# The S5 Toeplitz matrix of a hybrid mixer, laid out by DMAs that shift partitions in place of matmuls with shift matrices

## The chip, the cores and the metric

The kernel runs on one core of a Trainium2 chip. The metric is device time in microseconds of one execution, lower is better. The kernel before was timed three times: 862.27, 859.94 and 861.67 us, so its median is 861.67 us.

## What is computed

One layer of a hybrid block, batch 1, 512 tokens, width 1024, all in float32: an adaptive layer norm whose six rows come from `c @ w_ada`, an input projection, two branches (a four-head mLSTM and a 512-wide S5 state-space model), a gated mix, a second adaptive norm and a convolutional GLU of hidden width 2816. The change lies in the S5 branch alone:

```python
def _s5_ssm(u, lam_re, lam_im, log_dt, b_re, b_im, c_re, c_im, d):
    ...                                   # ar, ai = exp(lam*dt); bb = B scaled by (a-1)/lam
    bu_r = einsum('bsgc,gpc->bsgp', ug, bbr)          # 32 groups of 16 channels, 64 states
    bu_i = einsum('bsgc,gpc->bsgp', ug, bbi)
    ...                                   # x[s] = a * x[s-1] + bu[s], complex, along the 512 tokens
    y = einsum('gcp,bsgp->bsgc', c_re, xr) - einsum('gcp,bsgp->bsgc', c_im, xi)
    return y.reshape(B, S, W) + d * uf
```

The kernel cuts the 512 tokens into 64 blocks of 8. Inside a block the answer to the block's own inputs is a product with a block-Toeplitz matrix, whose 16x16 blocks are K[t-s] = C A^(t-s) B for t >= s and zero otherwise.

## The kernel before

Every large product (input projection, GLU of the S5 branch, mLSTM down projection, mix, FFN up and down) runs as three fp32r matmuls: `mm3` (L241 to L244) multiplies the high part of the weights with the high and the low part of the activations, and the low part of the weights with the high part. A weight tile of 128x1024 is loaded by SP into tag `w` (2 buffers), rounded to fp32r by ACT into `wh` (L221, through `split_into`), and the rest goes into `wl` by a DVE subtraction (L210). One such tile makes 24 matmuls of 512 columns.

The mixer stage is a list of tokens, `SEQ` (L144 to L150), written out by hand: `k` is one step of the first projection, `u x o g l d` a weight tile of 24 matmuls, `S` one step of the S5 stream and `H` one step of the mLSTM head stream. So S5 and head work is interleaved with weight tiles. Python order gives the priority; a list scheduler then orders the instructions of each engine at build time, so an instruction of a later token can stand a few places ahead of one that is not ready. On the chip each engine takes its own instructions strictly in that order. SP issues all DMAs, in one order.

The S5 stream is `s5_scalars`, and then for each quarter q of the groups `s5_params(q)` and `s5_run(q)`:

- `s5_params`, by S steps. (1) load B and C, build AB by DVE products (`cmul`). (2) G = AB transposed. (3) K: 16 matmuls (L523), an ACT copy (L524), a transpose (L525), an ACT cast into K high (L527) and a DVE subtraction into K low (L210); then the Toeplitz matrix TT: for each of 8 rows t one 0/1 shift matrix of 128x128 times K high and K low (L534, L535), into two PSUM banks of tag `s5`, each emptied by an ACT copy (L536). (4) F by DVE products. (5) E, the powers for the scan, by DVE and POOL.
- `s5_run`: (6) eight DMAs write the inputs into U (L575 to L577, shown as L192). (7) G times U (L583), a scan on DVE. (8) products on DVE into XB, then py = F times XB (L612) plus TT times U (L614), and an ACT copy (L617). (9) eight DMAs back (L621, L622), the skip term and gelu.

The shift matrices are an input of 512 KB (`in_shift`), loaded once and cast once by ACT (L501), and they hold one of the five `s5b` buffers until the fourth TT. TT is first read at L614, five S steps after it is made. The tiles of tag `s5b` (5 buffers) in a quarter are AB, G, TT and F.

Of the kernel before, what the change touches and what calls it, by code (L numbers as in the profile page):

```python
# [16 lines left out]
P = 128  # L17
# [37 lines left out]
def pack(i):  # L55
    f = np.float32
    a = {k: np.asarray(v) for k, v in i.items()}
    o = {}
    o["x"] = a["x"][0]
    wa = a["w_ada"][0].reshape(KD, P, 6, KD, P)  # L60
    o["wa1"] = wa[:, :, [1, 0]].transpose(3, 1, 0, 2, 4).reshape(KD, P, KD * 2 * P)
    o["wa2"] = wa[:, :, [4, 3, 2, 5]].reshape(KD, P, 4 * D)
    perm = np.arange(S).reshape(4, KD, C5).transpose(0, 2, 1).reshape(-1)
    w_in = a["w_in"][0]
    b_in = a["b_in"][0]
    o_i = 2 * D
    o_us = o_i + 8
    o_ga = o_us + S
    gg = np.arange(2 * D).reshape(2, KD, P).transpose(1, 0, 2).reshape(-1) + o_ga
    order = np.concatenate([o_us + perm, np.arange(o_i), gg])  # L70
    wt = w_in[:, order].reshape(KD, P, 36, P)
    bmain = b_in[order]
    o["w0"] = wt[:, :, :NXM0].reshape(KD, P, NXM0 * P)
    o["win"] = wt[:, :, NXM0:].transpose(2, 1, 0, 3).reshape(36 - NXM0, P, D)
    wg = np.zeros((KD, P, 32), f)
    wg[:, :, :8] = w_in[:, o_i:o_us].reshape(KD, P, 8)
    o["wg"] = wg.transpose(1, 0, 2).reshape(P, KD * 32)
    wq = a["w_mlstm_q"][0].reshape(2, 2, 2, P, QK)
    wk = a["w_mlstm_k"][0].reshape(2, 2, 2, P, QK)
    o["wqk"] = np.stack([wq, wk], 2).transpose(0, 4, 1, 2, 3, 5).reshape(2, P, D)  # L80
    o["wdn"] = a["w_mlstm_down"][0].reshape(KD, P, KD, P).transpose(2, 1, 0, 3).reshape(KD, P, D)
    o["wglu"] = a["w_s5_glu"][0][perm].reshape(4, P, 2, KD, P).transpose(3, 1, 2, 0, 4).reshape(KD, P, D)
    o["wmix"] = a["w_mix_out"][0].reshape(KD, P, D)
    o["wup"] = a["w_ffn_up"][0].reshape(KD, P, 2, NF, P).transpose(3, 2, 1, 0, 4).reshape(2 * NF, P, D)
    o["wfd"] = a["w_ffn_down"][0].reshape(NF, P, D)
    cols = np.zeros((P, NCOLS), f)

    def put(name, v):
        s, n = COLS[name]
        cols[:, s:s + n] = v  # L90

    ada = a["b_ada"][0].reshape(6, KD, P)
    put("c", a["c"][0].reshape(KD, P).T)
    put("ada1", ada[[1, 0]].transpose(2, 0, 1).reshape(P, 16))
    put("ada2", ada[[4, 3]].transpose(2, 0, 1).reshape(P, 16))
    put("b_in", bmain.reshape(36, P).T)
    put("b_gate", np.broadcast_to(b_in[o_i:o_us], (P, 8)))
    put("cw", a["w_mlstm_conv"][0].reshape(4, KD, P).transpose(2, 0, 1).reshape(P, 32))
    put("cb", a["b_mlstm_conv"][0].reshape(KD, P).T)
    put("gain", a["mlstm_norm_gain"][0].reshape(KD, P).T)  # L100
    put("d", a["s5_d"][0][perm].reshape(4, P).T)
    put("fw", a["w_ffn_conv"][0].reshape(3, NF, P).transpose(2, 0, 1).reshape(P, 66))
    put("fb", a["b_ffn_conv"][0].reshape(NF, P).T)
    o["rows"] = np.stack([ada[2].reshape(-1), ada[5].reshape(-1), a["ln1_gain"][0], a["ln1_bias"][0],
                          a["ln2_gain"][0], a["ln2_bias"][0]])
    lam = np.zeros((P, 3, NG), f)
    lam[:, 0] = a["s5_lam_re"][0].reshape(NG, P).T
    lam[:, 1] = a["s5_lam_im"][0].reshape(NG, P).T
    lam[:, 2] = np.repeat(a["s5_log_dt"][0].reshape(NG, 2).T, N5, 0)
    o["lam"] = lam.reshape(P, 3 * NG)  # L110
    bc = np.stack([np.stack([a["s5_b_re"][0], a["s5_b_im"][0]]),
                   np.stack([a["s5_c_re"][0], a["s5_c_im"][0]]).transpose(0, 1, 3, 2)])
    o["s5bc"] = bc.reshape(2, 2, 4, 4, P, C5).transpose(4, 2, 0, 1, 3, 5).reshape(P, 4, 256)
    o["ident"] = np.eye(P, dtype=f)
    mk = np.zeros((P, 16), f)
    mk[np.arange(16), np.arange(16)] = 1.0
    mk[32 + np.arange(16), np.arange(16)] = 1.0
    put("mask", mk)
    sg = np.zeros((P, 8), f)
    for j in range(8):  # L120
        sg[j::32, j] = 1.0
    put("selg", sg)
    o["cols"] = cols
    sh = np.zeros((P, T5, P), f)
    for t in range(T5):
        for s in range(t + 1):
            for q in range(C5):
                sh[(t - s) * C5 + q, t, (T5 - 1 - s) * C5 + q] = 1.0
    o["shift"] = sh.reshape(P, T5 * P)
    return {k: np.ascontiguousarray(v) for k, v in o.items()}  # L130


# [26 lines left out]
def _build(ctx, tc, nc, h):  # L159
# [19 lines left out]
    def big(shape=(P, D), dt=F32, tag="hb"):  # L179
        return tl(tag, shape, dt)  # L180
# [304 lines left out]
        tt(dst, x, c[:, 0:1, g4][:, :, :, None].to_broadcast([P, 2, 4, m]))  # L485
        tt(dst, dst, t, ALU.add)

    shr = [None]

    def s5_params(q, out):  # L490
        g4 = slice(4 * q, 4 * q + 4)
        bc = s5h()
        dma(bc[:, :256], h["s5bc"][:, q, :])
        b4 = bc.rearrange("p (x r a c) -> p x r a c", x=4, r=2, a=4)
        bt, ct = b4[:, 0], b4[:, 1]
        cb = bc[:, 256:].rearrange("p (r a c) -> p r a c", r=2, a=4)
        if shr[0] is None:
            s_ = big(tag="s5b")
            dma(s_, h["shift"])
            shr[0] = big((P, T5, P), F32R, "s5b")  # L500
            A.copy(shr[0].rearrange("p a b -> p (a b)"), s_)  # L501
        AB = big((P, 2, 4, P), tag="s5b")
        cmul(AB[:, :, :, :C5], bt, prm["z"], g4, False, C5)
        for i, a_ in enumerate(prm["apow"]):
            n = C5 << i
            cmul(AB[:, :, :, n:2 * n], AB[:, :, :, :n], a_, g4, False, n)
        yield
        gts(ct[:, 1], ct[:, 1], -1.0)
        GP.memset(cb, 0.0)
        GP.tensor_copy(cb[0:64, :, :, 0:C5], ct[0:64])  # L510
        GP.tensor_copy(cb[64:P, :, :, C5:32], ct[64:P])
        G = big((P, 2, 4, P), tag="s5b")
        for ri in range(2):
            pg = bank("s5")
            for i in range(4):
                T.transpose(pg[:, i * P:(i + 1) * P], AB[:, ri, i, :], ident)
            A.copy(G[:, ri].rearrange("p a b -> p (a b)"), pg)
        yield
        kt = s5h(P)
        pk = bank("s5")  # L520
        for ri in range(2):
            for i in range(4):
                T.matmul(pk[32 * i:32 * i + 32, :P], lhsT=cb[:, ri, i, :], rhs=AB[:, ri, i, :], start=ri == 0, stop=ri == 1)  # L523
        A.copy(kt, pk[:, :P])  # L524
        T.transpose(pk[:, P:2 * P], kt, ident)  # L525
        K = s5h(256, F32R).rearrange("p (a b) -> p a b", a=2)
        A.copy(K[:, 0, :], pk[:, P:2 * P])  # L527
        sub(K[:, 1, :], pk[:, P:2 * P], f32(K[:, 0, :]))
        TT = big((P, 8, T5, C5), tag="s5b")
        for b in range(2):  # L530
            pq = bank("s5")
            for i in range(4):
                o = pq[:, i * P:(i + 1) * P]
                T.matmul(o, lhsT=shr[0][:, 4 * b + i, :], rhs=K[:, 0, :], start=True, stop=False)  # L534
                T.matmul(o, lhsT=shr[0][:, 4 * b + i, :], rhs=K[:, 1, :], start=False, stop=True)  # L535
            A.copy(TT[:, :, 4 * b:4 * b + 4, :], pq.rearrange("p (t g c) -> p g t c", t=4, c=C5))  # L536
        yield
        F = big((P, 2, 4, P), tag="s5b")
        cmul(F[:, :, :, :C5], ct, prm["apow"][0], g4, True, C5)
        for i, a_ in enumerate(prm["apow"]):  # L540
            n = C5 << i
            cmul(F[:, :, :, n:2 * n], F[:, :, :, :n], a_, g4, True, n)
        yield
        E = s5h().rearrange("p (r g k) -> p r g k", r=2, k=K5)
        t = s5h().rearrange("p (r g k) -> p r g k", r=2, k=K5)
        lo8, hi8 = prm["e8"]
        E5, t5 = (x.rearrange("p r g (i l) -> p r g i l", l=8) for x in (E, t))
        for ri in range(2):
            lv = [lo8[:, k, g4, None, :].to_broadcast([P, 4, 8, 8]) for k in (ri, 1 - ri)]
            hv = [hi8[:, k, g4, :, None].to_broadcast([P, 4, 8, 8]) for k in range(2)]  # L550
            tt(E5[:, ri], lv[0], hv[0])
            tt(t5[:, ri], lv[1], hv[1])
            tt(E[:, ri], E[:, ri], t[:, ri], ALU.add if ri else ALU.subtract)
        rho = s5h().rearrange("p (r g k) -> p r g k", r=2, k=K5)
        GP.tensor_copy(rho, prm["m8"][:, None, g4, None].to_broadcast([P, 2, 4, K5]))
        GP.memset(rho[:, :, :, 0:1], 0.0)
        out[q] = (TT, G, F, E, rho)
        yield
# [698 lines left out]
```

## Time and profile before

| what | value |
|---|---|
| timed runs (device time) | 862.27, 859.94, 861.67 us, median 861.67 us |
| span of the profiled execution | 862.0 us |
| PE busy | 828.5 us (96%), 4106 matmuls |
| DVE busy | 607.1 us (70%) |
| ACT busy | 368.6 us (43%) |
| POOL busy | 98.0 us (11%) |
| mean granted TensorE clock | 0.994 |
| HBM traffic | 101.01 MB read, 2.10 MB written |

The profiled execution has its span and no other time of its own; the span stands 0.33 us above the median of the timed runs, inside their spread, so nothing measurable lies around it. PE's 96% is a share over the whole span, and matmuls are pipelined; so what PE waits for, and which engine the chain of work runs through, has to be read stretch by stretch. The S5 quarters lie between about 60 and 300 us.

### The profile page before, as it was taken

The numbers are of one execution on the slowest core, as the hardware profiler recorded it, in microseconds if no ns is written. First come the engines' busy times: TensorE is split into PE (matmuls) and PEld (weight loads), VectorE is DVE, ScalarE is ACT, GpSimd is POOL, SyncE is SP. The second block draws the span as 40 slices with busy tenths as digits, with TensorE's granted clock in tenths as the row PEclk, the third lists the DMA queues.
The fourth block names the chain that finished last, engine by engine and source line by source line (L and its number), as shares of the span: only waits on it lengthen the run. The fifth ranks groups of instructions, "written<-read, shape, count | busy, mean of one in ns | idle before, by whom it ended". The sixth has DMA issues, their size and how long they took to land.

```text
span 862.0 us, 11353 instructions
## 1 busy us (share of the span) xinstructions
PE 828.5 (96%) x4106; PEld 669.2 (78%) x4106; DVE 607.1 (70%) x1144; ACT 368.6 (43%) x589; POOL 98.0 (11%) x255
## 2 busy tenths in 40 slices
PE   3999999999999999999999999999999999999996
PEld 1777868778777778888887988888888878888785
DVE  5557978788689774578978767556777675878144
ACT  4454573564556442232334555444444444333000
POOL 2781211122022100000002200000000000000000
PEclk9999999999999999999999999999999999999998
DMA  9832132122222233568655023224444232445011
GB/s 336 288 132 86 53 101 62 45 85 62 79 60 87 86 123 122 196 203 294 210 191 177 2 74 102 94 98 147 146 147 137 86 120 74 171 163 169 11 49 49
DMA packets 45415, 105.94 MB, mean 123 GB/s; under 512 B 13360, under 2 KB 14256, under 8 KB 45360
## 3 DMA queue, kind: packets, MB, share of 16 engines
q1 hardware_dynamic: 45360, 105.23, 36.0%
q8 instruction: 32, 0.52, 0.2%
q14 instruction: 23, 0.19, 0.1%
HBM read 101.01 MB, written 2.10 MB: 120 GB/s over the span
## 4 chain that ended last, share of the span: by engine, by line
PE 76%; DVE 11%; ACT 4%; DMA 4%; issue 2%; SPq 2%; POOL 0%; DVEq 0%; ACTq 0%; POOLq 0%
PE acc L242 11%; PE acc L243 11%; PE acc L244 11%; PE hd L242 11%; PE hd L243 11%; PE hd L244 11%; DVE hh L202 2%; SPq L192 2%; DVE s5h L207 1%; PE s L242 1%; PE s L244 1%; PE s L243 1%; DVE wl L210 1%; PE s L612 1%; DMA w<-in_wmix 1%
## 5 line engine op out<-in xcount | busy, mean ns | idle before, releaser
L221 ACT CAST wh<-w 128x1024 fp32r<-128x1024 f32 (+2 forms) x103 | 103.2, 1003 | 144.0 <-PE acc L243 111.5
L210 DVE TENSOR_TENSOR wl<-w,wh 128x1024 fp32r<-128x1024 f32 (+2 forms) x103 | 120.5, 1172 | 60.8 <-ACT wh L221 60.1
L242 PE MATMUL acc<-hp,wh 128*128 128x512 f32 x256 | 103.4, 405 | 0.5 <-ACT hx L785 0.5
L244 PE MATMUL acc<-hp,wl 128*128 128x512 f32 x256 | 102.1, 399 | 0.0
L243 PE MATMUL acc<-hp,wh 128*128 128x512 f32 x256 | 102.1, 399 | 0.0
L242 PE MATMUL hd<-s5b,wh 128*128 128x512 f32 (+1 forms) x168 | 63.4, 380 | 0.7 <-ACT s5b L1169 0.5
L243 PE MATMUL hd<-s5b,wh 128*128 128x512 f32 (+1 forms) x168 | 63.6, 379 | 0.2 <-DVE s5b L210 0.2
L244 PE MATMUL hd<-s5b,wl 128*128 128x512 f32 (+1 forms) x168 | 63.3, 378 | 0.0
L242 PEld LDWEIGHTS acc<-hp,wh 128*128 128x128 f32 x256 | 48.2, 189 | 14.7 <-issue 3.7
L202 DVE SCALAR_TENSOR_TENSOR hh<-hh,hh 128x512 f32<-128x512 f32 x52 | 35.9, 691 | 31.2 <-ACT hh L564 14.7
L244 PEld LDWEIGHTS acc<-hp,wl 128*128 128x128 f32 x256 | 48.4, 189 | 11.2 <-issue 0.4
L243 PEld LDWEIGHTS acc<-hp,wh 128*128 128x128 f32 x256 | 48.4, 189 | 10.8 <-issue 0.4
L202 DVE SCALAR_TENSOR_TENSOR s5h<-hh,k,s5h 128x512 f32<-128x512 f32 x56 | 39.3, 746 | 4.7 <-DMA hh<-in_wa 4.6
L242 PEld LDWEIGHTS hd<-s5b,wh 128*128 128x128 f32 x168 | 31.3, 188 | 7.6 <-ACT s5b L1169 0.8
L243 PEld LDWEIGHTS hd<-s5b,wh 128*128 128x128 f32 x168 | 31.7, 189 | 7.0 <-DVE s5b L210 0.6
L244 PEld LDWEIGHTS hd<-s5b,wl 128*128 128x128 f32 x168 | 31.6, 188 | 6.4
L202 DVE SCALAR_TENSOR_TENSOR hh<-hh,k,hh 128x512 f32<-128x512 f32 x44 | 33.0, 751 | 4.5 <-ACT hh L1186 3.6
L1024 POOL TENSOR_SCALAR mov<-mov 128x1 f32<-128x1 f32 x6 | 3.7, 624 | 276.2 <-ACT s L1023 159.6
L244 PE MATMUL acc<-hx,wl 128*128 128x512 f32 x84 | 33.1, 394 | 0.0
L242 PE MATMUL acc<-hx,wh 128*128 128x512 f32 x84 | 33.1, 394 | 0.0
L243 PE MATMUL acc<-hx,wh 128*128 128x512 f32 x84 | 33.1, 394 | 0.0
L244 PE MATMUL acc<-s5b,wl 128*128 128x512 f32 x80 | 31.6, 395 | 0.5 <-DVE wl L210 0.5
(547 smaller groups left out, 2053.1 us busy)
## 6 DMA issues: line engine op xcount, KB each, us to landing
w<-in_wup SPq DMA_DIRECT2D x44, 512.0 KB, 3.2
hh<-in_wa SPq DMA_DIRECT2D x64, 256.0 KB, 4.2
w<-in_win SPq DMA_DIRECT2D x30, 512.0 KB, 3.2
w<-in_wfd SPq DMA_DIRECT2D x22, 512.0 KB, 3.3
hb<-in_wa SPq DMA_DIRECT2D x16, 512.0 KB, 7.4
w<-in_wglu SPq DMA_DIRECT2D x8, 512.0 KB, 3.3
w<-in_wdn SPq DMA_DIRECT2D x8, 512.0 KB, 3.3
w<-in_wmix SPq DMA_DIRECT2D x8, 512.0 KB, 4.2
```

What stands on the lines that cost most here:

```text
L192: return nc.sync.dma_start(o, i)
L202: V.scalar_tensor_tensor(o, i0, s, i1, op0=op0, op1=op1)
L207: V.tensor_tensor(o, a, b, op=op)
L210: V.tensor_tensor(o, a, b, op=ALU.subtract)
L221: A.copy(hi, x)
L242: T.matmul(o, lhsT=wh, rhs=xh, start=first, stop=False)
L243: T.matmul(o, lhsT=wh, rhs=xl, start=False, stop=False)
L244: T.matmul(o, lhsT=wl, rhs=xh, start=False, stop=last)
L612: T.matmul(o, lhsT=F[:, ri, pr, :], rhs=XB[:, ri, pr].rearrange("p g k -> p (g k)"), start=ri == 0, stop=False)
L1024: GP.tensor_scalar(v[:, 2:3], v[:, 0:1], v[:, 1:2], EPS * D, op0=ALU.add, op1=ALU.add)
```

## The change

The shift input, its load, its cast and the 64 matmuls with it are gone. K is now one plain float32 tile (no high and low part). For each t an SP DMA copies rows 0 to 127-z of K to rows z to 127 of a new tile TR at place t, with z = 16(7-t), and POOL zeroes the first z rows (seven memsets a quarter, none for t = 7). Then the S step ends (the `yield` stands behind the DMAs), and the next S step begins with one ACT copy of 128x1024 from TR into TT, which changes the order of the free dimensions from (t, group, channel) to (group, t, channel), and goes on with F. The number of S steps is the same. TR is a fifth `s5b` tile of a quarter, in the place of the shift matrices' buffer.

```diff
-    sh = np.zeros((P, T5, P), f)
-    ...
-    o["shift"] = sh.reshape(P, T5 * P)
...
-        if shr[0] is None:
-            s_ = big(tag="s5b")
-            dma(s_, h["shift"])
-            shr[0] = big((P, T5, P), F32R, "s5b")
-            A.copy(shr[0].rearrange("p a b -> p (a b)"), s_)
...
-        K = s5h(256, F32R).rearrange("p (a b) -> p a b", a=2)
-        A.copy(K[:, 0, :], pk[:, P:2 * P])
-        sub(K[:, 1, :], pk[:, P:2 * P], f32(K[:, 0, :]))
+        K = s5h(P)
+        A.copy(K, pk[:, P:2 * P])
+        TR = big((P, T5, 8, C5), tag="s5b")
+        for t in range(T5):
+            z = (T5 - 1 - t) * C5
+            if z:
+                GP.memset(TR[0:z, t], 0.0)
+            dma(TR[z:P, t].rearrange("p g c -> p (g c)"), K[0:P - z, :])
+        yield
         TT = big((P, 8, T5, C5), tag="s5b")
-        for b in range(2):
-            pq = bank("s5")
-            for i in range(4):
-                o = pq[:, i * P:(i + 1) * P]
-                T.matmul(o, lhsT=shr[0][:, 4 * b + i, :], rhs=K[:, 0, :], start=True, stop=False)
-                T.matmul(o, lhsT=shr[0][:, 4 * b + i, :], rhs=K[:, 1, :], start=False, stop=True)
-            A.copy(TT[:, :, 4 * b:4 * b + 4, :], pq.rearrange("p (t g c) -> p g t c", t=4, c=C5))
-        yield
+        A.copy(TT.rearrange("p g t c -> p t g c"), TR)
```

## Rows read from the trace of the kernel before

**Rows 1.** Busy time by stretch: length, then PE, PEld, DVE, ACT, POOL, clock, DMA, GB/s.
```profile
100.00:150.00 50.00, 48.41 (x274) 39.52 (x274) 42.55 (x101) 25.72 (x46) 9.27 (x23) 1.00 0.26 82
...
300.00:350.00 50.00, 49.47 (x214) 39.35 (x215) 29.97 (x41) 18.65 (x24) 0.00 (x0) 1.00 0.36 122
```

**Rows 2.** Who PE waited for, whole span: total us, times, longest us.
```profile
PE s L612 <- DVE k L210: 3.3, 3, 1.7
```

**Rows 3.** The shift matmuls by line, and two pieces of the chain of work through them.
```profile
L535 PE MATMUL s<-s5h,s5b x32: 223/274/327, 67.0 to 252.4; 128*128 128x128 f32 x32
...
67.23 0.11 PE s L534
```

**Rows 4.** ACT by line: the two copies out of PSUM in each quarter.
```profile
L536 ACT COPY s5b<-s x8: 581/587/590, 67.9 to 253.3; 128x512 f32<-128x512 f32 x8
```

**Rows 5.** DMA issues: size of each, median us from issue to landing.
```profile
w<-in_win SPq DMA_DIRECT2D x30, 512.0 KB, 3.2
...
s5h<-hx SPq DMA_DIRECT2D x32, 32.0 KB, 2.1
...
s5b<-in_shift SPq DMA_DIRECT2D x1, 512.0 KB, 5.8
```

**Rows 6.** SP's issues in order of time, by start and length.
```profile
67.42 5.83 SPq L192 DMA_DIRECT2D s5h<-hx  x8
...
295.27 1.95 SPq L192 DMA_DIRECT2D hh<-in_wa  x4
```

**Rows 7.** What SP's queue and ACT's weight casts waited for, whole span.
```profile
SPq L192 <- DVE wl L210: 427.5, 89, 36.0
...
ACT wh L221 <- PE acc L243: 111.5, 39, 5.8
```

**Rows 8.** POOL in order of time: a memset of 64 columns.
```profile
67.92 0.15 POOL L671 MEMSET hh<- 128x64 f32 x1
```

**Rows 9.** DVE in order of time, first quarter; in brackets the idle time before.
```profile
66.54 0.29 DVE L210 TENSOR_TENSOR s5h<-s,s5h 128x128 fp32r<-128x128 f32 x1 [0.50 <-ACT s5h L527]
...
74.98 0.19 DVE L652 TENSOR_TENSOR k<-hd,k 128x32 f32<-128x32 f32 x1 [0.49 <-PE hd L650]
```

**Rows 10.** ACT in order of time, first quarter.
```profile
69.31 1.20 ACT L769 ACTIVATE hx<-hd,k 128x512 f32<-128x512 f32 x1
...
73.10 0.59 ACT L647 COPY hh<-hd 128x512 f32<-128x512 f32 x1 [0.36 <-PE hd L645]
79.51 1.05 ACT L221 CAST wh<-w 128x1024 fp32r<-128x1024 f32 x1 [5.83 <-PE acc L243]
```

**Rows 11.** Second quarter, DVE in order of time.
```profile
129.52 0.29 DVE L202 SCALAR_TENSOR_TENSOR hh<-hd,hh 128x128 f32<-128x128 f32 x1 [0.66 <-POOL hh L854]
...
144.06 1.29 DVE L207 TENSOR_TENSOR hh<-hd,hx 128x512 f32<-128x512 f32 x2 [0.16 <-PE hd L891]
```

**Rows 12.** Second quarter, PE in order of time: the wait ahead of L612.
```profile
161.61 0.46 PE L612 MATMUL s<-k,s5b 128*128 128x128 f32 x2 [1.65 <-DVE k L210]
```

**Rows 13.** Third quarter: DVE in order of time, then PE ahead of L612.
```profile
190.32 0.29 DVE L210 TENSOR_TENSOR s5h<-s,s5h 128x128 fp32r<-128x128 f32 x1 [0.25 <-ACT s5h L527]
...
202.51 1.29 DVE L207 TENSOR_TENSOR hh<-hd,hx 128x512 f32<-128x512 f32 x2 [0.42 <-PE hd L891]
...
222.67 0.73 PE L612 MATMUL s<-k,s5b 128*128 128x128 f32 x4 [1.24 <-DVE k L210]
```

**Rows 14.** Fourth quarter: DVE, then PE, in order of time.
```profile
250.68 0.72 DVE L198 TENSOR_SCALAR hh<-hh,mmv,ms 128x256 f32<-128x256 f32 x2
...
253.47 1.08 DVE L210 TENSOR_TENSOR s5b<-hx,s5b 128x512 fp32r<-128x512 f32 x1 [0.68 <-ACT s5b L221]
...
252.54 0.63 PE L891 MATMUL hd<-k,hh 128*128 128x128 f32 x4
```

**Rows 15.** Busy time behind two waits ahead of L612; clock third from the end.
```profile
163.00:166.00 3.00, 3.00 (x16) 3.00 (x16) 2.98 (x4) 0.00 (x0) 0.00 (x0) 0.50 0.06 12
...
222.00:224.00 2.00, 1.33 (x11) 1.36 (x12) 1.96 (x5) 0.00 (x0) 0.00 (x0) 1.00 0.66 250
```

## What the change will do to the time, predicted before it ran

> **What bounds the kernel now.** I read the busy time by stretch first. Between 100 and 150 us PE is busy 48.4 of 50 us and DVE 42.6; between 300 and 350 us PE 49.5 and DVE 30.0 [rows 1]. So PE is the bound, but in the S5 stage DVE stands close behind it, while later it doesn't. Then the list of PE's waits: the one of the S5 stage that returns is L612, which waits for the last DVE subtraction into XB, 3.3 us in three waits [rows 2]. There PE has run out of work that it may do before DVE is through. That decides how this change is to be costed: PE work that is taken away in front of such a wait comes back as a longer wait, unless the DVE work in between starts earlier too. So for each quarter I follow DVE from the shift matmuls to L612 and look for the idle time that PE had caused. Only that idle time, and work that leaves DVE itself, can be won.
>
> **What is removed from PE.** 32 matmuls on L534 and 32 on L535, one every 0.11 us in the chain of work [rows 3]: 64 x 0.11 = 7.0 us, 1.76 us in each quarter. This is the ceiling of the gain from PE.
>
> **Where it arrives, quarter by quarter.** The low part of K leaves DVE too: one subtraction of some 0.2 to 0.3 us a quarter.
> - First quarter. DVE waits 0.50 us for the cast of K (L527) and then subtracts; both go, and F starts 0.7 us earlier. From there DVE works without a break on F, E and a weight tile until L652 of the gates, ahead of which it idles 0.49 us waiting for PE [rows 9]. With PE 1.8 us earlier that wait goes too. Gain 0.7 + 0.5 = 1.2 us.
> - Second quarter. From 129.52 us DVE is busy with F, E, the statistics of the head and weight tiles, and the only idle time on the way to L612 that ends with PE is 0.16 us, before 144.06 [rows 11]. Gain 0.16 us; PE's wait ahead of L612 grows from 1.65 us [rows 12] to about 3.2.
> - Third quarter. The wait for the cast (0.25 us) and the subtraction (about 0.2) go, and the 0.42 us in which DVE waits for PE's L891 [rows 13]. Gain 0.9 us; the wait ahead of L612 grows from 1.24 us [rows 13] to about 2.1.
> - Fourth quarter. The last four transposes of L891 start at 252.54 us, behind the shift matmuls, though DVE had made their input by 250.68 + 0.72 = 251.40 [rows 14]: PE could win 1.1 us, and 0.3 more by the missing subtraction. DVE idles 0.68 us behind an ACT cast that had stood behind L536 [rows 14]; with the subtraction that is 1.0 us. I take the smaller, 1.0 us, since DVE is full behind it.
>
> Sum: 1.2 + 0.16 + 0.9 + 1.0 = 3.3 us. After 300 us PE has no such neighbour, and what was won stays won.
>
> **What goes at no price.** The load of 512 KB (5.8 us to landing [rows 5]) and its one cast on ACT lie ahead of the first quarter, in a stretch where PE works on; I book nothing, at most some tenths of a microsecond. The two PSUM banks of tag `s5` a quarter come free earlier; nothing.
>
> **What is added.** (1) SP: 8 issues a quarter. The trace has no such DMA. The nearest issues from SBUF to SBUF, U's, take 5.83 us for eight [rows 6], 0.73 each; plain loads take 1.95 us for four, 0.49 each [rows 6]. So 3.9 to 5.8 us of SP a quarter, and the landing 2.1 us behind the last issue [rows 5]. The first waits for the copy of K; behind it in SP's queue stand U's eight DMAs and the next weight loads. In the first quarter U would be issued from about 71 us on in place of 67.42, but L583 reads it at 87. The weight loads have room: SP stood 427 us in all waiting for DVE to free a `w` buffer, and the casts waited 111 us for PE to free `wh` [rows 7], so a load that starts 4 us later is still early. I book nothing; a price of up to 1 us in all stays in the range.
>
> (2) ACT: one copy of 128x1024 in place of two of 0.587 us [rows 4]. A cast of the same size took 1.05 us [rows 10], so 1.05 to 1.2 us against 1.17: nothing. But it waits for the DMAs, and ACT takes its work in order. In the first quarter K is there at 66.5 us [rows 9], the last DMA lands between 66.5 + 7 x 0.49 + 2.1 = 72.0 and 66.5 + 7 x 0.73 + 2.1 = 73.7 us. Behind the copy could stand L769 (69.31), L647 of the gates (73.10) and, after an idle stretch of 5.8 us, the cast at 79.51 [rows 10]. If the copy stands in that idle stretch it costs nothing, and since TT is read only near 101 us, that is where I put it. If it stands just ahead of L647, it holds the gates until 73 to 75 us and the 1.2 us of the first quarter are lost, with up to 1.7 more. I take nothing, and keep both ends.
>
> (3) POOL: seven memsets a quarter of 128 columns. 64 columns took 0.15 us [rows 8], so 0.2 to 0.3 us each, 1.4 to 2.1 us a quarter. DVE does wait for POOL's masks at times (0.66 us before 129.52 [rows 11]); if memsets fall just there, some of it is added: 0 to 1 us in all.
>
> The Trainium skill speaks against such a change: "DMA: Bandwidth & Descriptors", Rules for kernel authors, says to coalesce many small transfers, since under 64 KB one pays mostly overhead. The trace agrees as far as it goes: 32 KB land in 2.1 us and 512 KB in 3.2 [rows 5]. By that rule alone the 32 DMAs would be all latency; it turns into time only if someone waits for them, which is the second rival.
>
> **The sum.** 861.67 - 3.3 = 858.4 us. The sum is made against a span of 862.0 us (858.7 after it); the median lies 0.33 us below the span, so I subtract from the median. With the unknown costs of SP, POOL and ACT the forecast's own range is 857.5 to 861.
>
> **The rivals.**
> - The whole PE time arrives: 861.67 - 7.0 = 854.7 us. It needs DVE's order to move so that the head and scan operations come ahead of F and E, which nobody needs until L612 and the scan. The scheduler could do that, since PE would hand over the heads' results earlier. For it: F and E stand between in all quarters. Against it: in the second quarter DVE is full whatever the order.
> - Slower: the copy into TT stands on ACT right behind the copy of K, and ACT stands still for the DMAs. In the first quarter that holds ACT from 66.5 to 73.7 us, then the copy, so L769, which empties the PSUM bank for the gates' matmuls, starts at 74.8 in place of 69.31 [rows 10]. PE has no other work ready between the last step of the first projection and the gates, and loses 5.5 us less the idle time of its own, about 4.9; the other three quarters still bring 0.16 + 0.9 + 1.0 = 2.1. That gives 861.67 + 4.9 - 2.1 = 864.5 us; if the same happens in the second quarter, where ACT's exponentials lead to POOL's masks and DVE [rows 11], 4 to 5 us more, 869. It decides as soon as the copy stands ahead of L769 there. For it: the two S steps of the first quarter follow each other without a token between. Against it: U's and the back DMAs' readers wait little, so the scheduler knows roughly how long eight DMAs take.
> - The clock: the waits ahead of L612 grow to 2 and 3 us. After the wait of 1.65 us in the second quarter the granted clock was 0.50, the 1.2 GHz level, through the stretch from 163 to 166 us, where 16 matmuls took 3.0 us [rows 15], 0.19 each in place of 0.11 [rows 3]; after the 1.24 us of the third it stayed at 1.00 [rows 15]. One more such stretch costs about half of 3.4 us, 1.7 us: 858.4 + 1.7 = 860.1, two 861.8 us.
> - It doesn't do what it says: no case for that; the matmuls are gone from the program.
>
> On the clock the Trainium skill ("TensorE: Matmul & The Clock Gate", HAM oscillation) says that idle gaps of PE take the clock to half and that this cost is paid anew for each. The rows agree for one gap and not for the other [rows 15]; what a gap of 2 us does is shown by none.
>
> **Chances.** Forecast (857.5 to 861, most of it under 859.1) 0.42; whole PE time (853.5 to 857) 0.2; clock 0.17; ACT stands still (863 to 870) 0.13; small losses that leave 859 to 862, 0.08. The likeliest time is 858.4. The range leaves out the deep end of the slower case and little of the fast one: 854 to 863 us. A measurement of this kernel tells about 0.3%, 2.6 us, from no change: faster means below 859.1, slower above 864.3. Faster: 0.42 x 0.75 + 0.2 = 0.52; slower 0.11; the rest, 0.37, the same.
>
> **What would show it.** Right: PE busy falls by about 7 us; PE's waits for DVE at L612 grow from 3.3 us to some 6 to 7; L652 of the gates comes 1 to 2 us earlier, and the stage after the fourth quarter about 3 us earlier. ACT's copy into TT starts without a wait of more than a microsecond or two. Wrong: L612's waits stay as they were and the S5 stage ends 6 to 7 us earlier (first rival); ACT idle for DMAs by 3 us or more ahead of the copy, with PE idle behind it (second); a second stretch of clock 0.50 between 60 and 300 us (third).

## The result, and the profile after

The changed kernel took 894.97 us (median, 893.20 to 895.72), the kernel before 861.08 us in the same comparison: a ratio of 1.039, 95% interval 1.0375 to 1.0404. So it is 33.9 us slower, where 858.4 us and a range up to 863 had been forecast.

The profiled execution of the changed kernel took 893.2 us and has a span of 891.2; some 2 us lie around the span. The prediction had the span of before alone and saw nothing around it. By spans the loss is 891.2 - 862.0 = 29.2 us; the rest of the 33.9 between the medians lies in how the two profiled executions stand to their medians. The next lines, both of the changed kernel, are the busy times and one stretch (length, PE, PEld, DVE, ACT, POOL, clock, DMA, GB/s).

```profile
PE 831.6 (93%) x4042; PEld 668.6 (75%) x4042; DVE 604.8 (68%) x1140; ACT 367.9 (41%) x584; POOL 101.9 (11%) x283
```

```profile
300.00:350.00 50.00, 30.65 (x140) 24.50 (x139) 25.19 (x50) 11.86 (x20) 1.27 (x2) 0.80 0.17 52
```

The 64 matmuls did go (4042 in place of 4106), yet PE is busy for 3.1 us longer. Between 300 and 350 us, where it had worked 49.5 of 50 us [rows 1], it works 30.7. In the whole span PE idles 891.2 - 831.6 = 59.6 us in place of 33.5: 26.1 more. That PE's busy time rose by 3.1 although some 7.0 us of matmuls are gone leaves 10.1 us for the lower clock: the granted clock stands at 0.50 for some 41 us between 40 and 360 us, before for 3.4, and PE works through 27 us of the 41. Half of that is lost, 13.3 us in place of 1.7: 11.6 more, near the 10.1. So the loss by spans is 26.1 us of idle time and 3.1 us of busy time. The list of PE's waits says whom it waited for (total us, times, longest):

```profile
PE hd L236 <- ACT s5b L215: 14.2, 2, 12.2
PE s L307 <- DVE hx L291: 12.8, 1, 12.8
PE hd L877 <- DVE hh L192: 6.0, 4, 3.8
PE s L598 <- DVE k L204: 4.2, 2, 3.4
```

L307 is the start of the kernel and waits as long before. L598 is the old L612 [rows 2]: 4.2 us, no great matter. L877 (the heads, old L891) had waited 1.8 us in all. New is the first line. It lies in the first part of the S5 branch's GLU, which needs the S5 outputs of all four quarters. Its products with the earlier quarters ran between 300.8 and 312.5 us; what PE stands for is the split of the fourth quarter's output, and it takes its work in order. On PE in order of time, and in two stretches around it:

```profile
333.46 0.79 PE L236 MATMUL hd<-s5b,wh 128*128 128x512 f32 x1 [12.24 <-ACT s5b L215]
```

```profile
323.00:333.00 10.00, 0.00 (x0) 0.00 (x0) 2.88 (x5) 1.90 (x3) 0.00 (x0) 0.50 0.45 131
333.00:340.00 7.00, 6.25 (x14) 4.56 (x15) 4.49 (x7) 2.58 (x4) 0.00 (x0) 0.51 0.00 0
```

PE pays twice: it stands for 12 us, and for the 7 us behind that it works at a granted clock of 0.51.

So the S5 stream is late. Where it loses time is seen by following one quarter. These are the starts in us of five events in the four quarters of both kernels, read from the timelines (K is its copy out of PSUM; F its first product; U's DMAs their first issue; then the first matmul on U, and py):

| | K | F | U's DMAs | matmul on U | py |
|---|---|---|---|---|---|
| before, q1 | 66.2 | 66.7 | 67.4 | 87.4 | 100.5 |
| before, q2 | 128.2 | 130.5 | 131.1 | 149.2 | 161.6 |
| before, q3 | 190.0 | 193.9 | 194.5 | 210.4 | 222.7 |
| before, q4 | 248.9 | 251.3 | 252.7 | 272.7 | 285.5 |
| after, q1 | 64.4 | 73.2 | 73.6 | 94.6 | 107.1 |
| after, q2 | 135.1 | 138.9 | 141.7 | 161.8 | 174.8 |
| after, q3 | 203.9 | 209.5 | 215.5 | 233.1 | 244.6 |
| after, q4 | 274.3 | 280.7 | 282.1 | 306.1 | 315.8 |

Up to the first K the changed kernel is ahead by 1.8 us. From then on each quarter takes 5 to 8 us longer from K to py (42.7 us in place of 34.3 in the first), and the quarters follow one another, so py is late by 6.6, 13.2, 21.9 and 30.3 us. F starts 4 to 9 us behind K where it had started 0.5 to 4. The second quarter of the kernel before, K on ACT and F's first product on DVE, and then that of the changed kernel on SP, ACT and DVE:

```profile
128.21 0.27 ACT L527 CAST s5h<-s 128x128 fp32r<-128x128 f32 x1
```

```profile
130.48 0.26 DVE L207 TENSOR_TENSOR s5b<-s5h,k 128x128 f32<-128x128 f32 x1
```

```profile
135.39 5.54 SPq L186 DMA_DIRECT2D s5b<-s5h  x8
...
141.73 5.11 SPq L186 DMA_DIRECT2D s5h<-hx  x8
```

```profile
135.10 0.27 ACT L514 COPY s5h<-s 128x128 f32<-128x128 f32 x1 [0.48 <-PE s L512]
142.49 1.05 ACT L523 COPY s5b<-s5b 128x1024 f32<-128x1024 f32 x1 [4.13 <-DMA s5b<-s5h]
```

```profile
138.95 0.28 DVE L201 TENSOR_TENSOR s5b<-s5h,k 128x128 f32<-128x128 f32 x1
```

K is copied at 135.10, SP issues the eight shifting DMAs until 140.93, ACT's copy into TT waits 4.13 us for them. F's first product, which reads only C and powers of A, starts at 138.95, and U's DMAs at 141.73. On the chip neither waits for the copy. They stand late in the order that the scheduler wrote.

### The profile page after: what moved, and what is told of

It reads as the page before. It is cut to its first block, busy times and chain, and to the rows that moved or that the text cites. A ratio compares the mean times of both kernels' runs of the same rounds, so it can differ in the third digit from the quotient of the medians.

```text
span 891.2 us, 11303 instructions
## 1 busy us (share of the span) xinstructions
PE 831.6 (93%) x4042; PEld 668.6 (75%) x4042; DVE 604.8 (68%) x1140; ACT 367.9 (41%) x584; POOL 101.9 (11%) x283
## 4 chain that ended last, share of the span: by engine, by line
PE 76%; DVE 10%; ACT 4%; DMA 3%; POOL 3%; SPq 2%; issue 2%; DVEq 0%; ACTq 0%
PE acc L236 12%; PE acc L238 12%; PE acc L237 12%; PE hd L236 10%; PE hd L237 10%; PE hd L238 10%; SPq L186 2%; POOL k L339 2%; PE s L236 1%; PE s L238 1%; PE s L237 1%; PE s L598 1%; DVE hh L196 1%; DVE wl L204 1%; DVE s5h L201 1%
## 5 line engine op out<-in xcount | busy, mean ns | idle before, releaser
L236 PE MATMUL acc<-hp,wh 128*128 128x512 f32 x256 | 104.6, 409 | 0.9 <-ACT hx L771 0.9
L237 PE MATMUL acc<-hp,wh 128*128 128x512 f32 x256 | 103.1, 403 | 0.2 <-DVE hp L204 0.2
L236 PE MATMUL hd<-s5b,wh 128*128 128x512 f32 (+1 forms) x168 | 64.6, 387 | 14.7 <-ACT s5b L215 14.2
L237 PE MATMUL hd<-s5b,wh 128*128 128x512 f32 (+1 forms) x168 | 64.9, 387 | 0.7 <-DVE s5b L204 0.7
L204 DVE TENSOR_TENSOR hb<-hh,hb 128x512 fp32r<-128x512 f32 (+3 forms) x42 | 25.4, 610 | 10.9 <-ACT hb L215 10.8
```

Of the source, the lines that this page charges most:

```text
L204: V.tensor_tensor(o, a, b, op=ALU.subtract)
L236: T.matmul(o, lhsT=wh, rhs=xh, start=first, stop=False)
L237: T.matmul(o, lhsT=wh, rhs=xl, start=False, stop=False)
```

## The experiments

**Theories.** H (held): F, E and U stand behind the copy into TT in the program, and TT and F take their buffers from one tag, `s5b`, in turn. The scheduler hands F's tile out only after TT's first write, which in the change is a copy that waits for eight DMAs; so it writes F, E and U late, and the S5 stream with them. Q (queue): SP's eight more issues hold U. A: ACT stands still at the copy, the prediction's second rival. The scheduler's own choices are not in a trace; H is judged by where F, U and py stand when one thing in the program is changed.

### The copy moved, in two ways

```diff
-        TT = big((P, 8, T5, C5), tag="s5b")
-        A.copy(TT.rearrange("p g t c -> p t g c"), TR)
         F = big((P, 2, 4, P), tag="s5b")
         cmul(F[:, :, :, :C5], ct, prm["apow"][0], g4, True, C5)
+        TT = big((P, 8, T5, C5), tag="s5b")             # e13 here; e1 the same two lines behind rho
+        A.copy(TT.rearrange("p g t c -> p t g c"), TR)
```

> Changed kernel, with the one ACT copy from TR into TT traced behind F, E and rho in place of ahead of F; the DMAs, the memsets and their queue stay. Theory H (held): F's tile of tag s5b is handed out only after TT's first write, and that write waits for the eight DMAs, so F, E and U come late in every quarter, 6 to 9 us each. Then this kernel has none of it: 855 to 860 us, py of the fourth quarter at 278 to 286 us in place of 315.8, no wait of PE for the split of the S5 outputs. Theory Q (queue): SP's eight more issues and landings ahead of U's eight make the loss: then it stays at 885 to 895 us. Theory A (ACT stands still for the DMAs): the copy comes later, when the DMAs have landed, so 855 to 865 too; this run doesn't tell A from H.

> Changed kernel with two lines moved: F's tile and the first of its products stand ahead of the copy into TT, all else of F behind it. H at its narrowest: it is F's first write alone that has to come ahead of TT's first write; 858 to 862 us as with the copy behind F, E and rho. If it is the copy's place ahead of F's other products, or ACT standing at it: 870 us or more.

Measured 859.86 us (ratio 0.9978, interval 0.9963 to 0.9993) and 859.55 us (0.9975, 0.9960 to 0.9990). The scheduler writes the same order of instructions for both, on all engines, so the second is a repeat of the first: for that order all that counts here is whether F's first write stands ahead of TT's. The whole loss is gone, with every DMA and the copy still there, and this kernel is 0.2% below the one before, near what the measurement can tell. In the second of them, the mended kernel from here on, on DVE, on SP, among PE's waits and by stretch:

```profile
52.64 0.29 DVE L201 TENSOR_TENSOR s5b<-s5h,k 128x128 f32<-128x128 f32 x1 [1.58 <-POOL s5h L334]
```

```profile
66.14 5.47 SPq L186 DMA_DIRECT2D s5b<-s5h  x8
71.72 4.50 SPq L186 DMA_DIRECT2D s5h<-hx  x7
```

```profile
PE acc L238 <- DVE wl L204: 4.1, 2, 3.6
PE s L598 <- DVE k L204: 2.0, 2, 1.4
```

```profile
300.00:350.00 50.00, 49.24 (x210) 38.88 (x209) 29.85 (x41) 17.98 (x23) 0.00 (x0) 1.00 0.43 148
```

F starts at 52.6 us in the first quarter, 13 us ahead of the copy of K, and in the others at 126.7, 185.2 and 244.3, 1.8 to 2.4 us ahead. py of the fourth quarter stands at 285.2 (before 285.5), and PE is full again from 300 us on. U's DMAs are issued at 71.72, later than before (67.42 [rows 6]), and the matmul on U starts at 88.0 all the same (before 87.4): that speaks against Q. It speaks against A too, since ACT stands still at the copy in this kernel as well, for 2.38 us in the first quarter and 3.46 in the third (in the changed kernel 2.17, 4.13, 1.89 and 1.36 in the four), and the loss is gone. The third quarter:

```profile
194.72 1.06 ACT L525 COPY s5b<-s5b 128x1024 f32<-128x1024 f32 x1 [3.46 <-DMA s5b<-s5h]
```

### The wait alone, in the kernel before

```diff
     TT = big((P, 8, T5, C5), tag="s5b")
+    A.copy(TT[:, 0, 0, 0:1], TR[:, 7, 0, 0:1])   # TR of tag gab, filled by the same DMAs
     for b in range(2):                            # the shift matmuls stay
```

> Kernel before, with its 64 matmuls, to which the memsets and the 32 shifting DMAs are added at the place where the change puts them, into a tile that nobody reads (tag gab). The order of PE's instructions is that of the kernel before. H: nobody waits for these DMAs, so 861 to 865 us (1 to 3 us for SP and POOL at most). Q: U's DMAs stand behind them in SP's queue all the same, so U and py are late: 875 to 890 us. A: 861 to 863 us.

> Kernel before with its 64 matmuls and, as in the earlier run, the 32 DMAs into a tile of its own; new is one ACT copy of one column from the place that the last DMA writes into TT, traced ahead of the matmuls, so that TT's first write waits for the DMAs as in the change. H: F's tile is held again, U comes some 30 us behind K in place of 21 to 24, and the whole loss is there although no matmul was removed: 885 to 900 us. Q and A: the DMAs cost no more than they did unread, and ACT stands still by 2 to 4 us a quarter at most: 862 to 875 us.

Measured 862.50 us with the DMAs unread (ratio 1.0009, 0.9991 to 1.0027), and 886.72 us (1.0288, 1.0273 to 1.0303) when one column of TT waits for them. 24 us for a copy of one column. The second kernel's copy on ACT in the first quarter, its F, and a stretch:

```profile
72.94 0.19 ACT L536 COPY s5b<-gab 128x1 f32<-128x1 f32 x1 [1.11 <-DMA gab<-s5h]
```

```profile
72.41 0.28 DVE L207 TENSOR_TENSOR s5b<-s5h,k 128x128 f32<-128x128 f32 x1
```

```profile
300.00:350.00 50.00, 41.99 (x188) 32.73 (x189) 28.31 (x44) 14.52 (x22) 0.00 (x0) 0.93 0.26 82
```

F starts 7.1 us behind the copy of K (65.3), in place of 0.5 before, and py of the fourth quarter comes at 311.0. ACT stood for 1.11 us there and for 8.8 us in all four quarters, and A alone falls short of 24 us. This is most of the change's loss, with no matmul removed.

### F freed without moving the copy

```diff
+        F = big((P, 2, 4, P), tag="s5b")
+        GP.memset(F[:, 0, 0, 0:1], 0.0)               # e2
+        A.copy(F[:, 0, 0, 0:1], K[:, 0:1])            # e5, in its place
+        A.copy(F[:, 0, 0, 0:1], ct[:, 0, 0, 0:1])     # e14, in its place
         TT = big((P, 8, T5, C5), tag="s5b")           # e7: no touch, tag="gab"
         A.copy(TT.rearrange("p g t c -> p t g c"), TR)
```

> Changed kernel with the copy into TT at its place ahead of F's products; the one addition is a POOL memset of one column of F's tile traced ahead of the copy, so that F's tile of tag s5b gets its slot before TT's. H: as with the copy moved away, 855 to 861 us. Q: 885 to 895 us. A: ACT still takes the copy at its place in the program and stands still for the DMAs, so 880 to 895 us.

> Changed kernel; F's tile is written first by an ACT copy of one column that needs K alone, traced just ahead of the copy into TT, which keeps its place ahead of F's products. In the run with a POOL memset in this role that memset stood on POOL behind the S5 scalars and DVE waited 8.5 us for it near 59 us, ahead of the first quarter; from K on each quarter ran as with the copy moved. H: without that wait 856 to 862 us, U 23 to 29 us behind K in every quarter. A (ACT stands still for the DMAs at the copy's place): 870 to 895 us.

> The kernel in which ACT touches F's tile first (873 us), with one operand changed: the touch reads a column of C, which is there early, in place of K. The copy into TT is where it was. If the 13 us between that kernel and the one with the copy moved came with the touch's wait for K (another order of the third and fourth quarter): 858 to 863 us. If they belong to the copy's place on ACT: 870 to 875 us.

> Changed kernel with one word changed: TT is a tile of tag gab in place of s5b; the copy stays ahead of F's products, the DMAs stay. H: F no longer takes its slot behind TT: 853 to 860 us, like the copy moved, or a little better, since the fourth quarter's tiles come free earlier. If it is the copy's place in the program order and not the slot that holds F: 885 to 895 us, as changed.

Measured: 866.04 us with a POOL memset as F's first write, 873.24 us with an ACT copy that reads K, 860.55 us (ratio 0.9974, 0.9957 to 0.9992) with the same copy reading C, 872.67 us with TT in another tag. Each gives back 21.7 us or more, with the copy into TT where the change has it, and the third gives back all: H at its full size. The other three lie 5 to 13 us above the ranges that H gave for them; they have prices of their own. The memset, on DVE:

```profile
59.36 0.29 DVE L201 TENSOR_TENSOR s5b<-s5h,k 128x128 f32<-128x128 f32 x1 [8.54 <-POOL s5b L523]
```

It stands on POOL behind the S5 scalars, and DVE waits 8.54 us for it ahead of the first K, whose matmuls start at 69.5 us in place of 63.0. From there each quarter runs as with the copy moved: the matmul on U comes 24.8, 23.4, 22.6 and 29.5 us behind K's matmuls, with the copy moved (behind rho) 24.8, 23.4, 22.9 and 28.9.

With the touch that reads K, F starts behind K (67.1, 129.4, 189.3, 252.5), and PE loses time, in the fourth quarter above all. Its longest wait is close to the mended kernel's (4.30 us, there 3.60), but the clock stays low for longer; on PE, and in a later stretch:

```profile
268.19 0.80 PE L238 MATMUL acc<-hp,wl 128*128 128x512 f32 x1 [4.30 <-DVE wl L204]
```

```profile
285.00:290.00 5.00, 4.87 (x18) 3.48 (x16) 4.36 (x10) 3.49 (x8) 0.98 (x3) 0.50 0.00 0
```

Summed from 40 to 360 us PE idles 16.4 us, with the copy moved 11.0, and the granted clock stands at 0.50 for 20.5 us, there 3.4. Half of what PE worked in it is lost, 9.4 us and there 1.7, so 7.7 us more. 5.4 + 7.7 = 13.1, and the times differ by 13.4. That it comes from the touch's reading K in place of C is shown; why the order that follows is that much worse is not.

With TT in tag `gab` F starts at 53.9 us, ahead of K, and py of the fourth quarter at 283.8, as in the mended kernel: what held F was the shared tag, not the copy's place. Of the 13 us over it 8.5 are idle time again (19.5 us) and 3.1 half clock (4.8 us lost in place of 1.7). PE's longest wait is for ACT's gate tile of that very tag. Just ahead of that tile ACT had waited 1.44 us for the copy into TT and made it in 1.04, so up to 2.5 us of this wait may be A's. PE, then ACT:

```profile
258.78 0.80 PE L236 MATMUL acc<-hp,wh 128*128 128x512 f32 x1 [5.72 <-ACT gab L781]
```

```profile
257.10 1.04 ACT L523 COPY gab<-s5b 128x1024 f32<-128x1024 f32 x1 [1.44 <-DMA s5h<-hx]
```

### Does ACT stand still?

```diff
         A.copy(F[:, 0, 0, 0:1], K[:, 0:1])            # as in e5
-        A.copy(TT.rearrange("p g t c -> p t g c"), TR)
+        GP.tensor_copy(TT.rearrange("p g t c -> p t g c"), TR)
```

> The kernel in which ACT touches F's tile first, with the one copy from TR into TT made by POOL in place of ACT, at the same place in the program. That kernel was at 873 us, 13 us above the one with the copy moved behind F, E and rho. A (part of the loss is that ACT stands at the copy for the DMAs and what stands behind it on ACT comes late, the emptying of a PSUM bank near 255 us above all): without the copy on ACT the 13 us go, 858 to 863 us; POOL's masks may come 1 to 3 us later. If the 13 us have another cause: 870 to 875 us.

Measured 875.97 us. With the copy off ACT nothing came back of the 13 us, which speaks against A; POOL is the dearer engine for it, 4.40 us in the third quarter and 3.2 on average where ACT took 1.05, so a small part may hide behind that.

```profile
199.43 4.40 POOL L525 COPY s5b<-s5b 128x1024 f32<-128x1024 f32 x1 [4.20 <-DMA s5b<-s5h]
```

### What the DMAs cost where nothing is held

```diff
-            dma(TR[z:P, t].rearrange(...), K[0:P - z, :])                # SP
+            GP.memset(TR[:, t], 0.0)          # e4 (copy as changed), e12 (copy as e1), e18 (as e13, and
+                                              #  A.copy(TR[:, 7].rearrange(...), K) for the last row)
+            dma(TT[z:P, :, t, :], K[0:P - z, :].rearrange(...))          # e10; e11: traced behind U's DMAs
+            nc.gpsimd.dma_start(TR[z:P, t]..., K[0:P - z, :])            # e15; e16: nc.scalar; copy as e1
                                               # e8: memsets, DMAs and copy traced behind U's DMAs
```

> The mended kernel (F's first product ahead of the copy into TT) without its 32 DMAs: POOL writes zeros to the rows of TR for t below 7, ACT copies K into the last row, so that the copy into TT still comes behind K; of the S5 output inside a block only that row is right. The DMAs' price where nothing is held: if they are hidden, as the kernel before with added DMAs said (0.8 us), 857 to 860 us; if U behind them in SP's queue costs, 853 to 856 us.

> Changed kernel without the 32 DMAs: eight POOL memsets a quarter write all of TR with zeros, so the part of the S5 output inside a block is left out; the copy into TT stays ahead of F. H: the copy waits for POOL alone, some 2 us, so 853 to 859 us: what the removed matmuls are worth without any DMA. Q and A: the same. Against the run with the copy moved it prices the DMAs where nobody is held by them: 0 to 3 us.

> The kernel with the copy behind F, E and rho (859.9 us), without its 32 DMAs: POOL writes zeros to all of TR, so the part of the S5 output inside a block is left out. What it gains is the price of the DMAs where nothing is held: the removal alone was priced at 3.3 us (858.4 us) to 7.0 us (854.7 us). Below 857 us: the DMAs cost 3 us or more; 858 to 860: they cost nothing and the removal is worth the smaller sum.

> Changed kernel with the memsets and the eight shifting DMAs traced behind U's eight DMAs, and the copy behind them. H: nothing of F, E and U waits for the DMAs, nor for SP's 5 us: 853 to 859 us, at most 2 us below the kernel with the copy alone moved. Q: what SP costs there is given back too, 3 to 6 us below that kernel, 853 to 856 us.

> Changed kernel without TR and without the ACT copy: POOL's memsets and the eight DMAs of a quarter write TT itself, in pieces of 16 floats, at the place where they stand in the change. TT's first write is a memset that waits for nothing, so F is not held (H), and ACT has no copy to stand at (A): both expect 855 to 861 us. Q (SP and the DMAs themselves cost): DMAs in pieces of 64 bytes take longer to issue or land, U stands behind them: 865 us or more.

> The same, with memsets and DMAs traced behind U's eight DMAs, so that U waits for none of them. H and A: 854 to 860 us. Q: clearly below the kernel with them ahead of U, by 3 us or more.

> The kernel with the copy behind F, E and rho (859.9 us); the 32 shifting DMAs are issued by POOL in place of SP, so that U's DMAs and the weights don't stand behind them. Q in its mild form (SP's 5 us a quarter hold U by some us): U of each quarter 2 to 4 us earlier, 855 to 858 us. H alone: SP's issues are hidden, 858 to 862 us.

> The same with the 32 DMAs issued by ACT. ACT is idle for more than half of the span, but takes its work in order: eight issues of some 0.6 us right behind the copy of K hold what stands behind them. H alone: 858 to 862 us; Q: 855 to 858 us; if ACT's place matters, 863 us or more.

Without the DMAs 860.68 us (0.9992, 0.9981 to 1.0003), with them 859.55: they cost nothing that shows in the time. They do cost the S5 stream something: without them py of the fourth quarter comes at 276.5 us, 8.7 us earlier than in the mended kernel, and the time is no shorter for it. So some lateness of the stream is hidden. The price is not known to better than some 3 us: between 40 and 360 us PE of the kernel without DMAs idles 2.8 us less and loses 3.3 us more to the lower clock. Two earlier kernels without DMAs took 870.34 us each and missed the expectation for a reason of their own. Their copy of zeros needs POOL alone, so it was written far ahead of K, and ACT stood at it while POOL worked off the S5 scalars; ACT, then PE of the first of the two:

```profile
61.75 1.04 ACT L520 COPY s5b<-s5b 128x1024 f32<-128x1024 f32 x1 [8.57 <-POOL s5b L517]
```

```profile
63.12 0.69 PE L315 MATMUL s<-k,hh 128*128 128x128 f32 x2 [8.19 <-ACT hh L310]
```

Those 8 us are lost before the S5 quarters begin, so these two price nothing. In the second of them ACT stands for 8.42 us.

The DMAs traced behind U's: 864.63 us. Straight into TT, without TR and the copy: 864.69 us traced ahead of U, 866.49 behind it. Issued by POOL: 862.41 us; by ACT: 868.60. Every one is slower than 859.55. The two that are traced behind U's don't try what they were meant to try: the scheduler still writes the shifting DMAs ahead of U's on SP, seven of eight in the first quarter and all in the others. The second quarter of the first of them:

```profile
127.10 5.03 SPq L186 DMA_DIRECT2D s5b<-s5h  x8
132.23 6.18 SPq L186 DMA_DIRECT2D s5h<-hx  x8
```

So Q is tried by the issues of POOL and ACT alone. With POOL issuing, U's DMAs start at 66.50 us in the first quarter, where the kernel with the copy moved has 71.32, and the matmuls on U come 0.7, 1.0, 2.7 and 7.5 us earlier; the time is no shorter (862.41 and 859.86 us). Straight into TT, Q expected 865 us or more and H 855 to 861; the time lies just under Q's, but in the first quarter U is hardly later than in the mended kernel (DMAs at 72.08, matmul at 88.3 us), and py of the fourth comes earlier (282.5), so Q's reason doesn't hold. With ACT issuing, its queue shows one price, in the first quarter:

```profile
66.14 5.58 ACTq L520 DMA_DIRECT2D s5b<-s5h  x8
71.76 1.05 ACT L215 CAST wh<-w 128x1024 fp32r<-128x1024 f32 x1 [4.56 <-issue]
```

The weight cast behind the eight issues starts 4.56 us late. The other four are 3 to 7 us above the mended kernel. For 866.49 us the lower clock accounts for most (6.5 us lost between 40 and 360 us, in the mended kernel 1.7); the cause in the other three is open.

### F first in the kernel before

```diff
+        F = big((P, 2, 4, P), tag="s5b")
+        cmul(F[:, :, :, :C5], ct, prm["apow"][0], g4, True, C5)
         TT = big((P, 8, T5, C5), tag="s5b")           # and the shift matmuls, as before
```

> Kernel before, matmuls and all, with F's tile and its first product traced ahead of TT's tile and the shift matmuls: the same two lines moved as in the mended kernel. In the kernel before F starts 0.5 to 4 us behind the copy of K, in the mended one 1 to 13 us ahead of it. If part of the mended kernel's 859.6 us comes from that and not from the removed matmuls, this kernel gains too: 855 to 860 us. If F's place ahead of K is worth nothing here: 861 to 863 us, and the mended kernel's 2 to 3 us are the matmuls'.

Measured 865.96 us (1.0054, 1.0041 to 1.0066): slower by 4 us. F does start at 52.0 us, so in the kernel before it hung on TT's first write too; only that write came soon. py of the fourth quarter comes 5 us earlier (280.3) and the kernel is slower all the same. By spans it is 2.4 us slower, and 2.0 of them are idle time of PE between 40 and 360 us (10.5 us, before 8.5); whom the order makes it wait for was not followed. An earlier F is worth nothing by itself there, so the mended kernel's gain is not F's alone. This kernel and the mended one differ by the change alone, with F first in both: 865.96 - 859.55 = 6.4 us, nearly all of PE's 7.0. Against the kernel before the mended one gains 1.9 to 2.7. So what the removal is worth depends on the order of instructions around it.

## Why the prediction was wrong, step by step

- **The failed step** is (2) of what is added, the copy on ACT. The step asked who needs the copy's result ("TT is read only near 101 us") and what stands behind it on ACT, put it into the idle stretch and booked nothing. On the chip it stands just there: ACT starts it at 71.69 us, after 2.17 us idle, and the gates' L638 (old L652) starts at 70.82, not later than before [rows 9]. What was not asked is what stands behind it in the program and shares its tag: F, and behind F come E and, two S steps on, U. Held by the copy in the order written, F starts 3.9 to 8.8 us behind K, and py of the fourth quarter comes 30.3 us late; with F's first write traced ahead the loss is gone (859.55 us). That wait is paid when the order is written, so the trace of before can't show it as a wait. What could be read there: DVE had idle time ahead of K, and yet F, which needs no K, starts at 66.7 us, 0.2 us after the subtraction of K [rows 9].
- **The second rival** (ACT stands still, 864.5 to 869 us) had the right event, the wait for the DMAs, and the wrong victim. The copies that it feared for came at 63.4 to 65.6 us (now L755), ahead of the copy into TT. Its price ended at 869 since it took one delay in one or two quarters; a delay of the S5 stream adds up over four, 30.3 us. ACT's standing explains little of it: the mended kernel has 5.8 us of it, the changed one 9.6.
- **PE's 7.0 us** are right as a ceiling: with the mend PE's busy time is 822.0 us against 828.5, 6.5 less, at 3.4 us of half clock in both.
- **3.3 us that arrive**: the mended kernel gains 1.9 to 2.7 us. That the size is near is luck, since its working does not hold, and between the two kernels with F first 6.4 us arrive, close to the first rival's price. L598 (old L612) waits 2.0 us, where 6 to 7 were forecast; the time comes back at other waits, the longest 3.6 us for a weight subtraction of a full DVE. The quarters don't come earlier by 1.2, 0.16, 0.9 and 1.0 us: py stands at 100.7, 162.9, 221.4 and 285.2, against 100.5, 161.6, 222.7 and 285.5.
- **SP**: eight issues took 5.5 us, 0.69 each, inside the forecast 3.9 to 5.8, and U's from 71.7 where "about 71" stood. Hidden, as booked; 0.8 us with the DMAs unread.
- **POOL**: 101.9 - 98.0 = 3.9 us busy for 28 memsets, 0.14 each, less than the 0.2 to 0.3 booked.
- **The clock**: no further stretch behind L598 in the mended kernel. In the changed one some 41 us stand at 0.50, 10 to 12 us of loss, behind waits that the prediction didn't have.
- **The page's rule**: the Trainium skill ("DMA: Bandwidth & Descriptors", Rules for kernel authors) speaks against many small transfers. The trace agrees: by size the small DMAs land 1.9 to 3.3 us after issue in the mended kernel, the 64 KB no later than the 8 KB, so mostly overhead. Where nothing was held behind them, 32 of them cost nothing that shows (859.55 against 860.68 us without). Where F was held behind the copy that waits for them, 33.9 us.

## What to carry to other kernels

When an instruction gets a new wait, ask not only who reads its result and what follows on its engine, but which tiles the scheduler can hand out only after it: what is traced behind it, out of the same tag. Trace the first write of a tile that is needed early ahead of a write that waits for DMAs; here one moved product was worth 35 us. In a chain that passes the same place four times, a delay adds up four times; ask then how much of the sum other work hides (here 8.7 us cost nothing that shows, and 30.3 us cost 29.2 by spans).

## What the runs showed of the hardware

- A long wait of PE cost twice: behind 12.24 us of idle PE worked for 7 us at a granted clock of 0.51. Shorter waits don't tell: behind the 1.65 us ahead of L612 in the kernel before the clock was 0.50 [rows 15], and behind the same wait, 1.66 us, in that kernel with the unread DMAs it was 1.00 (wait, then a stretch behind it):

```profile
158.90 0.46 PE L618 MATMUL s<-k,s5b 128*128 128x128 f32 x2 [1.66 <-DVE k L210]
```

```profile
160.00:163.00 3.00, 3.00 (x27) 2.97 (x27) 3.00 (x4) 0.21 (x2) 0.00 (x0) 1.00 0.02 5
```

- In two kernels whose longest waits in the S5 stage were 3.60 and 4.30 us the half clock stood for 3.4 us (copy moved) and for 20.5 us (touch that reads K).
- A DMA with pieces of 64 bytes to spread over SBUF (straight into TT) took SP as long as one with rows of 512: 5.58 us against 5.47 for eight issues.
